# Log-sum-exp over rows of 1024: two rows of the last sixteen are summed partly through the logarithm of an early part

## The chip, the cores and the metric

The kernel runs on one core of a Trainium2 chip. The metric is the device time of one execution in microseconds (us). Five engines of the core appear in the profile: TensorE (PE), VectorE (DVE), ScalarE (ACT), GpSimd (POOL) and SyncE (SP), which here issues all transfers of the normal path. Each engine works through its own list of instructions in order and waits on semaphores for the others. Sixteen DMA engines move the data.

## The reference

```python
x: float32 [32, 512, 1024], standard normal
max_x = np.max(x, axis=-1, keepdims=True)
out = max_x.squeeze(-1) + np.log(np.sum(np.exp(x - max_x), axis=-1))   # float32 [32, 512]
```

So there are 16,384 rows of 1024 numbers, 67 MB to read and 64 KB to write.

## The kernel before

The kernel leaves the maximum out: it sums `exp(x)` as it is and takes the logarithm. A guard then decides whether that was allowed: it checks that the sums lie between 1e-15 and 1e15, adds up what is out of bounds in `count` with small matmuls, and only if the check fails does a branch (`nc.If`) read everything again and compute with the maximum. Of the last piece of data the guard looks at the numbers themselves (none over 27), so that it need not wait for their sum.

**Layout.** Each of the 128 partitions has 128 rows. The first 112 (`W`) of a partition lie in one stretch of memory, the last 16 (`B`) in another. "Columns" are numbers of one partition: a row is 1024 columns. Data land in `ring`, which holds 48 rows of a partition.

**Loads.** `LOADS` lists 18 loads by size in rows and by what is done with them. All are issued by SyncE in this order on one queue (line 143); a load waits until those who used its place in the ring are done. Nine loads carry the first 112 rows. Nine smaller ones carry the last 16: 4576, 3328, 2528, 1856, 1344, 992, 736, 544 and 480 columns.

**Work on a load.** ScalarE takes the exponentials in place (line 235). Rows marked R are summed by VectorE (line 246). Rows marked F are first folded to half by GpSimd (line 240), and VectorE sums the halves (line 177). Rows marked T, those of the last sixteen but one, are summed on VectorE by one instruction a row, which adds its two halves and accumulates (line 256). The last row comes in two pieces, Y (544 columns) and Z (480). For both ScalarE writes the exponentials to PSUM and accumulates their sum itself (line 209), into `first_sum` and `last_sum`. VectorE copies the first sum to SBUF (line 219).

**The end.** The logarithms of the first 112 rows are taken in the middle of the tail (line 275) and stored by line 285. At the end come the logarithms of 15 rows (line 288) and that of the last row (line 290), which adds the two halves through the bias:

```python
    ln_last = act.did(nc.scalar.activation(
        out=res[:, LAST:NC], in_=last_sum, func=AF.Ln, bias=sumexp[:, LAST:NC]
    ))
```

Line 294 stores these 16 columns. Beside it VectorE and TensorE finish the guard (lines 299 to 317); ScalarE and VectorE read its verdict and tell SyncE, which then waits for the store and ends the program.

Of the kernel before, what the change touches and what calls it, by code (L numbers as in the profile page):

```python
# [16 lines left out]
B = 16  # L17
LATE = 119
AHEAD = 1
FIRST = 512  # L20

LOADS = [
# [3 lines left out]
]  # L29

# [24 lines left out]
def kernel(  # L55
# [22 lines left out]
    W = NC - B  # L78
    LAST = NC - 1
    x_rows = x_flat[0 : P * W].rearrange("(p c) d -> p (c d)", p=P)  # L80
# [12 lines left out]
    ]  # L93
    assert sum(size for size, _ in loads) == NC * d
    assert sum(s for _, ops in loads for _, s in ops) == NC

# [3 lines left out]
    ring = sbuf("ring", RING * d)  # L100
    sumexp = sbuf("sumexp", NC)
    res = sbuf("res", NC)
    clamped = sbuf("clamped", NC)
    bad = sbuf("bad", 3)
    over = sbuf("over", d)
    far = sbuf("far", 1)
    ones = sbuf("ones", 1)
    steep = sbuf("steep", 1)
# [3 lines left out]
    first_sum = nc.alloc_psum_tensor("first_sum", [P, 1], fp32).ap()  # L112
# [3 lines left out]
    landed = [nc.alloc_semaphore(f"landed{i}") for i in range(len(loads))]  # L116
    act = Counted(nc, nc.scalar, "act")
# [12 lines left out]
    dve.did(nc.vector.memset(steep, STEEP))  # L130
    less_at = dve.did(nc.vector.memset(less, -CEILING * (loads[-1][0] // 2)))


# [15 lines left out]
    def check_early():  # L149
        dve.wait(act, summed_by_act)  # L150
        dve.wait(dve, dve.n)
        dve.did(nc.vector.tensor_scalar(  # L152
            out=clamped[:, 0:LATE], in0=sumexp[:, 0:LATE],
            scalar1=LOW, scalar2=HIGH, op0=ALU.max, op1=ALU.min,
        ))
        dve.wait(dve, dve.n)
        dve.did(nc.vector.scalar_tensor_tensor(  # L157
            out=clamped[:, 0:LATE], in0=clamped[:, 0:LATE], scalar=0.0, in1=sumexp[:, 0:LATE],
            op0=ALU.bypass, op1=ALU.not_equal, accum_out=bad[:, 0:1],
        ))  # L160
# [3 lines left out]
    def add_up(c, who, **kw):  # L164
        pe.wait(*who)
        return pe.did(nc.tensor.matmul(count, lhsT=ones, rhs=sumexp[:, c : c + 1], **kw))  # L166

    folded = []

    def reduce_folded():  # L170

        nonlocal early_sum
        while folded:
# [15 lines left out]
    summed_by_act = 0  # L189
    ln_early = None  # L190
    first_loads = []
    for i, (size, ops) in enumerate(loads):
        if here + size > RING * d:
            assert here == p
            p = here = 0
        if any(q < here + size and q + t * d > here for _, t, q, _ in folded):
            reduce_folded()
        dma = load(i, here, done_before, size)
        if i < AHEAD:
            first_loads.extend(x.ins for x in dma)  # L200
        end = here + size
        done_before += size
        act.wait(landed[i], 16 * len(dma))
        for k, (how, s) in enumerate(ops):
            rows = ring[:, p : p + s * d].rearrange("p (c d) -> p c d", d=d)
            if how in "YZ":

                assert c == LAST and (how == "Z" or here == p)
                at = act.did(nc.scalar.activation(  # L209
                    out=last_exp[:, here - p : end - p], in_=ring[:, here:end], func=AF.Exp,  # L210
                    accum_out=first_sum if how == "Y" else last_sum,
                ))
                if how == "Z":
                    last_piece = ring[:, here:end]
                here = end
                if how == "Y":
                    nc.vector.addr_align(128, offset=0, max_nops=0)
                    dve.wait(act, at)
                    first_piece = dve.did(nc.vector.tensor_copy(out=sumexp[:, LAST:NC], in_=first_sum))  # L219
                summed_by_act = at  # L220
            elif how == "A":
                assert here == p
                v = ring[:, p : p + d]
                at = act.did(nc.scalar.activation(
                    out=v, in_=v, func=AF.Exp, accum_out=sumexp[:, c : c + 1]
                ))
                here += d
                users.append((p, p + d, act, at))
                summed_by_act = at
                who = (act, at)  # L230
            else:

                upto = end if k + 1 == len(ops) and c + s < LAST else p + s * d
                v = ring[:, here:upto]
                at = act.did(nc.scalar.activation(out=v, in_=v, func=AF.Exp))  # L235
                here = upto
            if how == "F":
                reduce_folded()
                pool.wait(act, at)
                at = pool.did(nc.gpsimd.tensor_tensor(  # L240
                    out=rows[:, :, 0:H], in0=rows[:, :, 0:H], in1=rows[:, :, H:d], op=ALU.add
                ))
                folded.append((c, s, p, at))
            elif how == "R":
                dve.wait(act, at)
                who = (dve, dve.did(nc.vector.reduce_sum(  # L246
                    out=sumexp[:, c : c + s], in_=rows, axis=AX.X
                )))
                users.append((p, p + s * d, *who))
            elif how == "T":  # L250
                if c >= W:
                    reduce_folded()
                dve.wait(act, at)
                for r in range(s):
                    lo = rows[:, r, 0:H]
                    who = (dve, dve.did(nc.vector.scalar_tensor_tensor(  # L256
                        out=lo, in0=lo, scalar=1.0, in1=rows[:, r, H:d],
                        op0=ALU.mult, op1=ALU.add, accum_out=sumexp[:, c + r : c + r + 1],
                    )))
                    users.append((p + r * d, p + (r + 1) * d, *who))  # L260
                    if c + r >= LATE:
                        add_up(c + r, who, start=False, stop=False)
            if how == "A" and c >= LATE:
                add_up(c, who, start=False, stop=False)
            if how in "RT":
                if c < W:
                    early_sum = dve.n
                reduce_folded()
            c += s
            p += s * d  # L270
            if c == LATE:

                act.wait(dve, early_sum)
                act.wait(act, early_act)
                ln_early = act.did(nc.scalar.activation(  # L275
                    out=res[:, 0:W], in_=sumexp[:, 0:W], func=AF.Ln
                ))
                check_early()
            if c <= W:
                early_act = summed_by_act  # L280
        assert here == end

# [4 lines left out]
    act.wait(dve, dve.n)  # L287
    act.did(nc.scalar.activation(out=res[:, W:LAST], in_=sumexp[:, W:LAST], func=AF.Ln))  # L288
    act.wait(act, summed_by_act)
    ln_last = act.did(nc.scalar.activation(  # L290
        out=res[:, LAST:NC], in_=last_sum, func=AF.Ln, bias=sumexp[:, LAST:NC]
    ))
    sp.wait(act, ln_last)
    nc.sync.dma_start(out=out_rest, in_=res[:, W:NC]).then_inc(stored, 16)

    dve.wait(dve, dve.n)
    dve.did(nc.vector.scalar_tensor_tensor(  # L299
        out=clamped[:, LATE:NC], in0=sumexp[:, LATE:NC], scalar=LOW,  # L300
        in1=sumexp[:, LATE:NC], op0=ALU.max, op1=ALU.not_equal, accum_out=bad[:, 1:2],
    ))
    add_up(LAST, (dve, first_piece), start=False, stop=False)
# [4 lines left out]
    half = last_piece.shape[1] // 2  # L308
    dve.wait(landed[-1], 16)
    dve.did(nc.vector.scalar_tensor_tensor(  # L310
        out=over[:, 0:half], in0=last_piece[:, 0:half], scalar=CEILING,
        in1=last_piece[:, half : 2 * half], op0=ALU.max, op1=ALU.max, accum_out=bad[:, 2:3],
    ))
# [119 lines left out]
```

## Time and profile before

| | |
|---|---|
| median of 3 runs | 161.55 us (161.47 to 161.6) |
| the profiled execution | 161.57 us |
| its span, first to last instruction | 160.2 us |
| busy: VectorE | 114.3 us (71%) |
| busy: ScalarE | 114.5 us (71%) |
| busy: GpSimd | 37.3 us (23%) |
| busy: TensorE | 2.2 us (1%) |
| HBM read | 67.11 MB, 419 GB/s over the span |

Times in the profile count from the first instruction of the span. The page gives each engine's busy time, the span in 40 slices, the chain of work that ended last, and the costliest groups of instructions by line, engine, operation and shape. An engine's idle time is put down to what ended it. Two instructions of one engine can overlap: the next one starts before the one ahead of it has written its last result, so the pace of an engine is read from start to start. "SPq" is the list of SyncE, where transfers are issued.

### The profile page before, as it was taken

To read this page: it belongs to the slowest core of one execution; us is meant where nothing else is said; L and a number is where in the kernel's file an instruction comes from. 1 tells how busy PE (TensorE), PEld (TensorE's weight loads), DVE (VectorE), ACT (ScalarE), POOL (GpSimd) and SP (SyncE) were. 2 spreads that over 40 slices of the span, in tenths; PEclk is the share of its full clock that TensorE was granted. 3 is DMA by queue.
4 is the path that set the end of the run, shared out by engine and by line. 5 is a ranking of instruction groups with operands and counts; after the bars stand their busy time and mean duration, and the time that the engine had idled before them with its cause. 6 is when DMAs were issued, how large, how long until landed. Compare 5 with 4: busy or idle time off the path is not lost.

```text
span 160.2 us, 221 instructions
## 1 busy us (share of the span) xinstructions
PE 2.2 (1%) x26; PEld 1.1 (1%) x26; DVE 114.3 (71%) x59; ACT 114.5 (71%) x31; POOL 37.3 (23%) x11
## 2 busy tenths in 40 slices
PE   0000000000000000000000000000000000000022
PEld 0000000000000000000000000000000000000011
DVE  0000000009999499994999859959999999999996
ACT  3000059980799708995099949992999989799996
POOL 0000000000000000000000994690004969891000
DMA  9996996996996996997999999999999999999992
GB/s 319 507 460 301 507 524 262 524 524 262 524 524 262 524 524 262 524 474 311 483 442 442 442 425 409 409 409 471 423 414 417 458 409 399 444 412 428 415 408 97
DMA packets 3025, 67.18 MB, mean 419 GB/s; under 512 B 592, under 2 KB 720, under 8 KB 1488
## 3 DMA queue, kind: packets, MB, share of 16 engines
q1 hardware_dynamic: 3024, 67.18, 97.8%
q14 instruction: 1, 0.01, 0.0%
HBM read 67.11 MB, written 0.07 MB: 419 GB/s over the span
## 4 chain that ended last, share of the span: by engine, by line
DMA 51%; ACT 28%; DVE 19%; issue 1%; PE 0%
DMA ring<-in_x_dram 51%; ACT ring L235 28%; DVE sumexp L246 16%; DVE sumexp L177 2%; DVE ring L256 1%; DVE over L310 0%; PE count L315 0%; ACT res L275 0%; DVE clamped L299 0%; DVE fine L317 0%; DVE sumexp L219 0%
## 5 line engine op out<-in xcount | busy, mean ns | idle before, releaser
L235 ACT ACTIVATE ring<-ring 128x16384 f32<-128x16384 f32 (+16 forms) x23 | 111.7, 4908 | 42.3 <-DMA ring<-in_x_dram 42.3
L246 DVE TENSOR_REDUCE sumexp<-ring 128x16 f32<-128x16384 f32 (+4 forms) x9 | 85.6, 9513 | 42.1 <-ACT ring L235 42.1
L240 POOL TENSOR_TENSOR ring<-ring 128x3072 f32<-128x3072 f32 (+3 forms) x7 | 37.1, 5315 | 107.2 <-ACT ring L235 107.2
L177 DVE TENSOR_REDUCE sumexp<-ring 128x6 f32<-128x3072 f32 (+3 forms) x7 | 18.4, 2659 | 0.0
L256 DVE SCALAR_TENSOR_TENSOR ring<-ring 128x512 f32<-128x512 f32 x15 | 9.6, 687 | 0.4 <-ACT ring L235 0.4
L127 ACT ACT_TABLE_LOAD x1 | 1.3, 1283 | 1.9 <-PEq L64 1.9
L162 PE MATMUL count<-far,bad 128*1 128x1 f32 x2 | 0.2, 164 | 153.0 <-DVE clamped L157 153.0
L166 PE MATMUL count<-sumexp,ones 128*1 128x1 f32 x18 | 1.6, 164 | 3.6 <-DVE ring L256 3.6
L128 DVE MEMSET ones<- 128x1 f32 x1 | 0.1, 59 | 2.0 <-PEq L64 2.0
L256 DVE DVE_READ_ACCUMULATOR ring<-ring 128x1 f32 x15 | 1.2, 82 | 0.0
L209 ACT ACTIVATE last_exp<-ring 128x544 f32<-128x544 f32 (+1 forms) x2 | 1.2, 588 | 0.0
L162 PEld LDWEIGHTS count<-far,bad 128*1 128x1 f32 x2 | 0.1, 82 | 153.0 <-DVE clamped L157 153.0
L166 PEld LDWEIGHTS count<-sumexp,ones 128*1 128x1 f32 x18 | 0.8, 81 | 4.4 <-DVE ring L256 4.4
L310 DVE SCALAR_TENSOR_TENSOR over<-ring 128x240 f32<-128x240 f32 x1 | 0.4, 404 | 0.0
L317 DVE TENSOR_SCALAR fine<-count 1x1 int32<-1x1 f32 x1 | 0.1, 147 | 0.3 <-PE count L315 0.3
L157 DVE SCALAR_TENSOR_TENSOR clamped<-clamped,sumexp 128x119 f32<-128x119 f32 x1 | 0.3, 283 | 0.0
L275 ACT ACTIVATE res<-sumexp 128x112 f32<-128x112 f32 x1 | 0.3, 279 | 0.0
L290 ACT ACTIVATE res<-last_sum,sumexp 128x1 f32<-128x1 f32 x1 | 0.3, 261 | 0.0
L209 ACT ACTIVATION_READ_ACCUMULATOR last_exp<-ring 128x1 f32 x2 | 0.3, 129 | 0.0
L152 DVE TENSOR_SCALAR clamped<-sumexp 128x119 f32<-128x119 f32 x1 | 0.2, 222 | 0.0
L288 ACT ACTIVATE res<-sumexp 128x15 f32<-128x15 f32 x1 | 0.2, 213 | 0.0
L299 DVE SCALAR_TENSOR_TENSOR clamped<-sumexp 128x9 f32<-128x9 f32 x1 | 0.2, 170 | 0.0
(17 smaller groups left out, 1.8 us busy)
## 6 DMA issues: line engine op xcount, KB each, us to landing
ring<-in_x_dram SPq DMA_DIRECT2D x1, 7936.0 KB, 21.3
ring<-in_x_dram SPq DMA_DIRECT2D x1, 6912.0 KB, 23.9
ring<-in_x_dram SPq DMA_DIRECT2D x1, 6400.0 KB, 19.7
ring<-in_x_dram SPq DMA_DIRECT2D x1, 4608.0 KB, 15.9
ring<-in_x_dram SPq DMA_DIRECT2D x1, 3584.0 KB, 24.0
ring<-in_x_dram SPq DMA_DIRECT2D x1, 3072.0 KB, 19.1
ring<-in_x_dram SPq DMA_DIRECT2D x1, 2288.0 KB, 24.2
ring<-in_x_dram SPq DMA_DIRECT2D x1, 1664.0 KB, 20.9
```

Of the source, the lines that this page charges most:

```text
L127: nc.scalar.preload_act_table_set("natural_log_exp_and_others")
L157: dve.did(nc.vector.scalar_tensor_tensor(out=clamped[:, 0:LATE], in0=clamped[:, 0:LATE], scalar=0.0, in1=sumexp[:, 0:LATE], op0=ALU.bypass ...
L162: pe.did(nc.tensor.matmul(count, lhsT=bad[:, 0:1], rhs=far, start=True, stop=False))
L166: return pe.did(nc.tensor.matmul(count, lhsT=ones, rhs=sumexp[:, c : c + 1], **kw))
L177: at = dve.did(nc.vector.reduce_sum(out=sumexp[:, c0 : c0 + s0], in_=halves, axis=AX.X))
L209: at = act.did(nc.scalar.activation(out=last_exp[:, here - p : end - p], in_=ring[:, here:end], func=AF.Exp, accum_out=first_sum if how == ...
L235: at = act.did(nc.scalar.activation(out=v, in_=v, func=AF.Exp))
L240: at = pool.did(nc.gpsimd.tensor_tensor(out=rows[:, :, 0:H], in0=rows[:, :, 0:H], in1=rows[:, :, H:d], op=ALU.add))
L246: who = (dve, dve.did(nc.vector.reduce_sum(out=sumexp[:, c : c + s], in_=rows, axis=AX.X)))
L256: who = (dve, dve.did(nc.vector.scalar_tensor_tensor(out=lo, in0=lo, scalar=1.0, in1=rows[:, r, H:d], op0=ALU.mult, op1=ALU.add, accum_out ...
L275: ln_early = act.did(nc.scalar.activation(out=res[:, 0:W], in_=sumexp[:, 0:W], func=AF.Ln))
L310: dve.did(nc.vector.scalar_tensor_tensor(out=over[:, 0:half], in0=last_piece[:, 0:half], scalar=CEILING, in1=last_piece[:, half : 2 * half ...
```

## The change

The nine loads of the last sixteen rows are cut anew: 3760, 3488, 2656, 2000, 1456, 1088, 800, 608 and 528 columns. The order is no longer that of the memory. The last load, 528 columns (`HEAD`), is the first part of row 0; the one before it, 608 columns (`BACK`), is the last part of row 15. The other part of row 0 (496 columns) comes with the first late load, and that of row 15 (416 columns) with the second. The fourteen rows between are summed by VectorE as before, each when its columns are there.

The early parts of rows 0 and 15 are summed by VectorE into `parts`. A small logarithm on ScalarE turns each into ln(sum / 2) and writes it twice next to the place where the last piece of its row lands (`joins`; a gap of 32 columns in the ring makes room). The exponentials of the last two pieces run over these two columns too, so that the accumulator gets the early sum back (twice a half) and adds the rest. The sum of row 15 goes to `sumexp`, that of row 0 to `last_sum` in PSUM; neither last logarithm has a bias. The copy of the first sum is gone. The code place of VectorE that is aligned (`addr_align`) now stands ahead of the halves of the 800-column piece.

```diff
-    (9, "R5 F4"), (7, "F4 R3"), (6, "F2 F2 R2"), (4.46875, "T4"), (3.25, "T3"), (2.46875, "T3"),
-    (1.8125, "T2"), (1.3125, "T1"), (0.96875, "T1"), (0.71875, "T1"), (0.53125, "Y"), (0.46875, "Z"),
+    (9, "R5 F4"), (7, "F4 R3"), (6, "F2 F2 R2"),
 ]
+HEAD, BACK, MID = 528, 608, 12
+PIECES = [2656, 2000, 1456, 1088, 800]
...
+    start = MID * d - sum(PIECES)
+    late = [(HEAD, start), (MID * d, B * d - BACK)]
+    for size in PIECES:
+        late.append((start, start + size))
+        start += size
+    late += [(B * d - BACK, B * d), (0, HEAD)]
...
+    def halves(v, c):
+        n = v.shape[1] // 2
+        return dve.did(nc.vector.scalar_tensor_tensor(
+            out=v[:, 0:n], in0=v[:, 0:n], scalar=1.0, in1=v[:, n : 2 * n],
+            op0=ALU.mult, op1=ALU.add, accum_out=c,
+        ))
...
+    gap = p + (B - MID) * d
+    def place(e0):
+        return e0 - MID * d + p if e0 >= MID * d else gap + GAP + e0
+    joins = bass.AP(
+        tensor=ring.tensor, offset=ring[:, gap : gap + 1].offset,
+        ap=[ring.ap[0], [GAP - 2, 2], [1, 2]],
+    )
+    for k, (s, e) in enumerate(late):
+        i = len(loads) + k
+        at0, at1 = place(s), place(s) + e - s
+        [dma] = load(i, at0, W * d + s, e - s)
+        act.wait(landed[i], 16)
+        if k >= len(late) - 2:
+            act.wait(act, joined)
+        if k == len(late) - 1:
+            head_sum = act.did(nc.scalar.activation(
+                out=last_exp[:, 0 : e - s + 2], in_=ring[:, at0 - 2 : at1], func=AF.Exp,
+                accum_out=last_sum,
+            ))
+            break
+        if k == len(late) - 2:
+            v = ring[:, at0 : at1 + 2]
+            back_sum = act.did(nc.scalar.activation(
+                out=v, in_=v, func=AF.Exp, accum_out=sumexp[:, NC - 1 : NC]
+            ))
+            sums.append((NC - 1, act, back_sum))
+            add_up()
+            continue
+        v = ring[:, at0:at1]
+        at = act.did(nc.scalar.activation(out=v, in_=v, func=AF.Exp))
...
+        if k == len(late) - 3:
+            nc.vector.addr_align(128, offset=0, max_nops=0)
+        dve.wait(act, at)
+        seen.append((s, e))
...
+        if k == 0:
+            halves(ring[:, at0 : place(0) + d], parts[:, 1:2])
+        if k == 1:
+            halves(ring[:, place((B - 1) * d) : at1], parts[:, 0:1])
+            both = dve.n
+            act.wait(dve, early_sum)
+            ln_early = act.did(nc.scalar.activation(
+                out=res[:, 0:W], in_=sumexp[:, 0:W], func=AF.Ln
+            ))
+            check_early()
+        if k >= 1:
+            add_up()
+        if k == 2:
+            act.wait(dve, both)
+            joined = act.did(nc.scalar.activation(
+                out=joins, in_=parts[:, :, None].to_broadcast([P, 2, 2]), func=AF.Ln, scale=0.5
+            ))
...
     act.wait(dve, dve.n)
-    act.did(nc.scalar.activation(out=res[:, W:LAST], in_=sumexp[:, W:LAST], func=AF.Ln))
-    act.wait(act, summed_by_act)
-    ln_last = act.did(nc.scalar.activation(
-        out=res[:, LAST:NC], in_=last_sum, func=AF.Ln, bias=sumexp[:, LAST:NC]
+    act.wait(act, back_sum)
+    act.did(nc.scalar.activation(out=res[:, W + 1 : NC], in_=sumexp[:, W + 1 : NC], func=AF.Ln))
+    act.wait(act, head_sum)
+    act.did(nc.scalar.activation(out=res[:, W : W + 1], in_=last_sum, func=AF.Ln))
```

More of the change, by code (lines that the diff above doesn't have):

```diff
@@ L93 @@
     ]
-    assert sum(size for size, _ in loads) == NC * d
-    assert sum(s for _, ops in loads for _, s in ops) == NC
+    assert sum(size for size, _ in loads) == W * d
+    assert sum(s for _, ops in loads for _, s in ops) == W
+    start = MID * d - sum(PIECES)
[4 more added lines that the diff above has]
+    late += [(B * d - BACK, B * d), (0, HEAD)]
+    assert start == MID * d and sum(e - s for s, e in late) == B * d
     def sbuf(name, cols, dtype=fp32, rows=P):
@@ L130 @@
     dve.did(nc.vector.memset(steep, STEEP))
-    less_at = dve.did(nc.vector.memset(less, -CEILING * (loads[-1][0] // 2)))
+    less_at = dve.did(nc.vector.memset(less, -CEILING * (HEAD // 2)))
     users = []
@@ L162, in check_early, with add_up @@
         pe.did(nc.tensor.matmul(count, lhsT=bad[:, 0:1], rhs=far, start=True, stop=False))
-    def add_up(c, who, **kw):
-        pe.wait(*who)
-        return pe.did(nc.tensor.matmul(count, lhsT=ones, rhs=sumexp[:, c : c + 1], **kw))
+    sums = []
+    def add_up():
+        while sums:
+            c, who, at = sums.pop(0)
+            pe.wait(who, at)
+            pe.did(nc.tensor.matmul(
+                count, lhsT=ones, rhs=sumexp[:, c : c + 1], start=False, stop=False
+            ))
     folded = []
@@ L205 @@
             rows = ring[:, p : p + s * d].rearrange("p (c d) -> p c d", d=d)
[L206 to L236, printed above, removed]
+            upto = end if k + 1 == len(ops) else p + s * d
+            v = ring[:, here:upto]
+            at = act.did(nc.scalar.activation(out=v, in_=v, func=AF.Exp))
+            here = upto
             if how == "F":
@@ L243 @@
                 folded.append((c, s, p, at))
-            elif how == "R":
+            else:
                 dve.wait(act, at)
[L246 to L267, printed above, removed]
+                at = dve.did(nc.vector.reduce_sum(out=sumexp[:, c : c + s], in_=rows, axis=AX.X))
+                users.append((p, p + s * d, dve, at))
+                early_sum = at
                 reduce_folded()
@@ L270 @@
             p += s * d
[L271 to L280, printed above, removed]
-        assert here == end
+        assert here == end
+    assert c == W and here == p and p + GAP + B * d <= RING * d
@@ new lines @@
+    gap = p + (B - MID) * d
[5 more added lines that the diff above has]
+    )
+    summed = set()
+    seen = []
+    for k, (s, e) in enumerate(late):
[12 more added lines that the diff above has]
+        if k == len(late) - 2:
+            assert at1 == gap
+            v = ring[:, at0 : at1 + 2]
[6 more added lines that the diff above has]
+        v = ring[:, at0:at1]
+        at = act.did(nc.scalar.activation(out=v, in_=v, func=AF.Exp))
+        if k == 0:
+            reduce_folded()
+        if k == len(late) - 3:
+            nc.vector.addr_align(128, offset=0, max_nops=0)
+        dve.wait(act, at)
+        seen.append((s, e))
+        for r in range(1, B - 1):
+            left = r * d
+            for s0, e0 in sorted(seen):
+                if s0 <= left < e0:
+                    left = e0
+            if r not in summed and left >= (r + 1) * d:
+                summed.add(r)
+                row = ring[:, place(r * d) : place(r * d) + d]
+                sums.append((W + r, dve, halves(row, sumexp[:, W + r : W + r + 1])))
+        if k == 0:
+            halves(ring[:, at0 : place(0) + d], parts[:, 1:2])
[13 more added lines that the diff above has]
+                out=joins, in_=parts[:, :, None].to_broadcast([P, 2, 2]), func=AF.Ln, scale=0.5
+            ))
```

35 lines of the change are left out of this document (16 added, 19 removed).

## The prediction

> **What bounds the kernel now.** I read the page first: is this kernel short of transfers or of an engine?
>
> ```profile
> span 160.2 us, 221 instructions
> ...
> DMA  9996996996996996997999999999999999999992
> ...
> DMA 51%; ACT 28%; DVE 19%; issue 1%; PE 0%
> ```
>
> The transfers are busy in nearly every slice, and in all of the second half. The change leaves the first nine loads as they are, so only what follows the six-row load matters. Hence the timeline of ScalarE, one instruction at a time, from there to the end:
>
> ```profile
> 138.06 1.91 ACT L235 ACTIVATE ring<-ring 128x2048 f32<-128x2048 f32 x1 [1.02 <-DMA ring<-in_x_dram]
> 141.68 1.89 ACT L235 ACTIVATE ring<-ring 128x2048 f32<-128x2048 f32 x1
> 143.51 4.02 ACT L235 ACTIVATE ring<-ring 128x4576 f32<-128x4576 f32 x1
> 147.44 2.98 ACT L235 ACTIVATE ring<-ring 128x3328 f32<-128x3328 f32 x1
> 150.33 0.28 ACT L275 ACTIVATE res<-sumexp 128x112 f32<-128x112 f32 x1
> 150.51 2.29 ACT L235 ACTIVATE ring<-ring 128x2528 f32<-128x2528 f32 x1
> 152.73 1.75 ACT L235 ACTIVATE ring<-ring 128x1856 f32<-128x1856 f32 x1
> 154.39 1.32 ACT L235 ACTIVATE ring<-ring 128x1344 f32<-128x1344 f32 x1
> 155.62 1.02 ACT L235 ACTIVATE ring<-ring 128x992 f32<-128x992 f32 x1
> 156.54 0.80 ACT L235 ACTIVATE ring<-ring 128x736 f32<-128x736 f32 x1
> 157.25 0.61 ACT L209 ACTIVATE last_exp<-ring 128x544 f32<-128x544 f32 x1
> 157.85 0.57 ACT L209 ACTIVATE last_exp<-ring 128x480 f32<-128x480 f32 x1
> 158.34 0.13 ACT L209 ACTIVATION_READ_ACCUMULATOR last_exp<-ring 128x1 f32 x1
> 158.39 0.21 ACT L288 ACTIVATE res<-sumexp 128x15 f32<-128x15 f32 x1
> 158.51 0.26 ACT L290 ACTIVATE res<-last_sum,sumexp 128x1 f32<-128x1 f32 x1
> ```
>
> From 138.06 ScalarE shows no idle time. That alone could mean that it is the bound. So I looked at when its data landed: the issues of SyncE in the timeline and, for the same loads, the time from issue to landing in the DMA view.
>
> ```profile
> 126.47 0.33 SPq L143 DMA_DIRECT2D ring<-in_x_dram  x1
> 135.53 0.33 SPq L143 DMA_DIRECT2D ring<-in_x_dram  x1
> 136.37 0.43 SPq L143 DMA_DIRECT2D ring<-in_x_dram  x1
> 136.85 1.54 SPq L143 DMA_DIRECT2D ring<-in_x_dram  x1
> 158.79 0.34 SPq L294 DMA_DIRECT2D out_dram<-res  x1
> ```
>
> ```profile
> ring<-in_x_dram SPq DMA_DIRECT2D x1, 272.0 KB, 20.8
> ring<-in_x_dram SPq DMA_DIRECT2D x1, 240.0 KB, 20.9
> out_dram<-res SPq DMA_DIRECT2D x1, 8.0 KB, 1.4
> ```
>
> The 544 columns landed at 136.37 + 20.8 = 157.17 and the last 480 at 136.85 + 20.9 = 157.75; their exponentials started at 157.25 and 157.85. So the two race: ScalarE is under 0.1 us behind the transfers. Does it keep its own pace? Two groups of the table by form give it:
>
> ```profile
> L235 ACT ACTIVATE ring<-ring 128x16384 f32<-128x16384 f32 x3 | 41.6, 13856 | 29.6 <-DMA ring<-in_x_dram 29.6
> L235 ACT ACTIVATE ring<-ring 128x4576 f32<-128x4576 f32 x1 | 4.0, 4017 | 0.0
> ```
>
> (13.856 - 4.017) / 11,808 columns is 0.8333 ns per column. From start to start 736 columns took 157.25 - 156.54 = 0.71 us, 0.10 over the columns; the log of 112 took 0.18, 0.09 over. I take a step as 0.8333 ns per column + 0.095 us. With an accumulator it is 0.147 over: 157.85 - 157.25 = 0.60 for 544. By this the 1856 columns could have started at 150.51 + 2.20 = 152.71 and did at 152.73; 1344, at 154.37 and did at 154.39. Transfers and ScalarE are tied within some 0.02 us at every step; gaining on one alone gains nothing.
>
> The last store is issued at 158.79, right behind the last log (158.51 + 0.26 = 158.77), and lands 1.4 later, at 160.2: the end of the span. The page's chain ends on VectorE's guard, which I check against SyncE's waits:
>
> ```profile
> SPq L376 <- ACTq L373: 0.7, 1, 0.7
> SPq L378 <- SPq L378: 0.3, 1, 0.3
> ```
>
> After its issue (158.79 + 0.34) SyncE waits 0.7 for the guard's verdict, then 0.3 for the store. So the guard has 0.3 us to spare. The profiled execution took 161.57 us, 1.33 over its span, and 0.02 over the median of 161.55. 0.2% of that, 0.32 us, is about what a measurement of this kernel can tell from no change.
>
> **The change part by part.** *Loads.* The last sixteen rows were nine loads of 4576, 3328, 2528, 1856, 1344, 992, 736, 544 and 480 columns; they become nine of 3760, 3488, 2656, 2000, 1456, 1088, 800, 608 and 528. Bytes and number are the same, so I cost the last landing at nothing: 157.75. The new first piece lies about four rows further along the ring, and waits for the reduction behind the 126.47 issue; the fifth piece now carries the wait behind the 135.53 issue. Their cover is the queue: nothing of the late pieces can move before the six-row load is in (138.06), 11 us later. Without that cover a late issue would delay every landing one for one.
>
> *Where the pieces start.* Before, four of nine pieces (3328, 2528, 736 and 480) start 128 bytes past a multiple of 256; after, six do not start at one (64, 128, 192, 128, 128 and 128 past), and a gap of 128 bytes shifts seven destinations against their sources. From one start on ScalarE to the next is what the later piece took to arrive, as the two are tied: 147.44 - 143.51 = 3.93 us for the 3328, 1.18 ns per column, and 0.92 for the 736, 1.25; beside them 2.22 for 1856 columns that start at a multiple, 1.20, and 1.23 for 992, 1.24. The shifted ones do not stand out, so I take nothing. The Trainium skill ("DMA: Bandwidth & Descriptors", "How a descriptor splits into AXI transactions") says that a read that does not begin at a multiple of 256 bytes also fetches the bytes from that boundary on, and pays for them. By it the starts wasted 4 x 128 = 512 bytes per partition before and 64 + 192 + 4 x 128 = 768 after, 32 KB more in all, an estimate of 0.08 us at the rate of the late pieces (8.39 MB in 19.7 us): a rule against the change, which the rows above don't bear out.
>
> *ScalarE's list.* Interpolating ScalarE's starts by columns gives when each new piece is there: 3760 at 142.54, then 146.67, 149.87, 152.27, 154.05, 155.40, 156.40, and from the two landings 157.11 and 157.75 (with 0.03 to start). Its list: the three 2048s of the six-row load end their steps at 141.68 + 1.80 = 143.48, so the 3760 wait 0.9 us for ScalarE. Then steps of 3.23 (to 146.71), 3.00 (149.71), the early log 0.19 (149.90), 2656 in 2.31 (152.21), the new small log 0.10 (152.31), 2000 in 1.76 (154.07), 1456 in 1.31 (155.38; data 155.40), 1088 in 1.00 (156.40), 800 in 0.76 (157.16), and 610 with an accumulator in 0.508 + 0.147 (157.82). Its data would be there at 157.78. So the last exponentials start at 157.82, 0.03 earlier than 157.85; they have 530 columns for 480, 0.04 more; accumulator read at 158.35 instead of 158.34.
>
> *The small log and its wait.* It stands in front of the 2000-column exponentials and waits for VectorE's sum of row fifteen's part. What is queued behind it is all that ScalarE still has to do. VectorE's rows:
>
> ```profile
> 146.38 1.22 DVE L177 TENSOR_REDUCE sumexp<-ring 128x2 f32<-128x1024 f32 x1
> 147.56 0.69 DVE L256 SCALAR_TENSOR_TENSOR ring<-ring 128x512 f32<-128x512 f32 x1
> 148.18 0.69 DVE L256 SCALAR_TENSOR_TENSOR ring<-ring 128x512 f32<-128x512 f32 x1
> 158.28 0.40 DVE L310 SCALAR_TENSOR_TENSOR over<-ring 128x240 f32<-128x240 f32 x1
> 158.60 0.08 DVE L310 DVE_READ_ACCUMULATOR over<-ring 128x1 f32 x1
> ```
>
> A row costs 0.62 us, 240 columns 0.32, so about 1.1 ns per column: 0.33 for the 248 of row zero, 0.29 for the 208 of row fifteen. Rows one to three and the part of row zero: 147.56 + 1.86 + 0.33 = 149.75. The 3488 end at 146.71 + 3.11 = 149.82; from 149.85 three rows and a part take 2.15, plus 0.08 for the accumulator: 152.08. ScalarE wants it at 152.21, so the wait costs nothing by 0.13 us. Its price is 0.10 as a step; from above it is bounded by the whole duration of the 112-column log, 0.28, if nothing overlaps it. I take 0.10, since that row's own step was 0.18. Below 0.09 it cannot go.
>
> *The 608's accumulator* now goes to the sums beside its row instead of PSUM: between 0 and one uncovered read, 0.13; I take 0, as the read before it overlapped. It also waits for two things, its data and the small log; ScalarE has no row for that. It is bounded by 0 and by the 0.08 from the landing at 157.17 to the start at 157.25; I take 0, the small log being 4.8 us old by then.
>
> *VectorE's end.* The copy of the first half's sum goes, and the last row's halves are those of the 800. The 1456's exponentials end at 154.07 + 1.21 + 0.20 = 155.48, and behind them four rows of 0.62 follow one another, the last two not held up by the 1088 (end 156.51) or the 800 (157.27): 157.96, with the read 158.04. The remaining logs want them at 158.40; the guard's final maximum starts no later than now (158.28) and is 24 columns, 0.03, longer. The 0.3 us of the guard hide this.
>
> *The last logs.* Fifteen columns at 158.40, the last one 0.12 later at 158.52. With the bias it took 0.26. The fifteen-column log without one took 0.21, of which 0.01 is columns: 0.20, a gain of 0.06. It could be 0, if reading the sum from PSUM is what costs; at most 0.10, as the exponentials that touch PSUM have the shortest fixed part (0.61 - 0.45 = 0.16). I take 0.06. The Trainium skill ("ScalarE: Activation LUTs", "What ACT_TABLE_LOAD costs") gives about 93 ns for a bias read per partition; by it the end would be 0.03 us earlier still.
>
> *Sum.* -0.03 (start) + 0.04 (columns) - 0.06 (bias) = -0.05 us: store issued at 158.74, span near 160.19, profiled execution 161.52, median 161.50.
>
> **The rivals.** *One: ScalarE's list grows* (slower). Its list and the landings tie, so whatever its steps cost more from 152.2 on comes out at the end one for one. Place: small log and 608. Price: small log not overlapped 0.18, accumulator 0.13, second wait 0.08, bias worth nothing 0.06: together 0.45, so 161.50 + 0.45 = 161.95. It passes 0.32 over the median when about 0.37 of this is real, or if VectorE's part is there after 152.6. For it: no row shows these forms, and ScalarE has no idle time to lose. Against: reads and short logs overlapped in every row.
>
> *Two: the starts cost* (the page's rule). Landing at 157.83, last start 157.86: 0.04 over the forecast, 161.54. Against: no misaligned row stands out.
>
> *Three: the transfers get faster,* from the shifted destinations. For it, the windows show room:
>
> ```profile
> 130.00:136.00 6.00, 0.00 (x0) 0.00 (x0) 6.00 (x3) 5.46 (x3) 5.70 (x2) 1.00 1.01 434
> 155.00:157.00 2.00, 0.61 (x8) 0.26 (x6) 1.97 (x7) 2.00 (x3) 0.00 (x0) 1.00 0.99 391
> ```
>
> The tail moves 391 GB/s where large pieces moved 434. The late pieces (16,384 columns of 4 bytes on 128 partitions, 8.39 MB) took 157.75 - 138.06 = 19.7 us; at 434 they take 19.3, 0.36 less. Against: ScalarE's list holds the start at about 157.8, so 161.48 is the price; a real gain of 0.36 (161.14) would need shorter steps as well. A fourth way, that the guard fails on the new sums and all is read again, would double the time; it gets 1%, counted with rival one.
>
> **How the numbers follow.** Forecast 0.63 (161.35 to 161.65: the three runs spread over 0.13, and single prices are uncertain by about 0.1). Rival one at its full size 0.20. Rival two 0.07, within 0.2%. Rival three 0.10, nearly all of the chance of faster, since it needs what no row shows. Faster by over 0.2%: 0.09. Within: 0.71. Slower: 0.20. The range goes from half of rival three's gain, 161.30, to just short of rival one's sum, 161.92.
>
> **What would show it.** Right: 530 columns starting near 157.82 with their read near 158.35; the small log near 152.2, starting without idle time and followed 0.10 later; the last log at 0.20; the store issued near 158.74. Wrong: idle time before the small log, with VectorE as its releaser; a step of the 610 columns above 0.66; the last landing away from 157.75; SyncE's last wait being the guard's and not the store's.

## The result, and the profile after

The changed kernel takes **161.99 us** in the median of ten runs (161.83 to 162.24), the kernel before 161.54 beside it (161.47 to 161.63, ten runs): a ratio of 1.0028, with a 95% interval of 1.0018 to 1.0037. It is slower by 0.45 us, where 161.50 with a range up to 161.92 was forecast.

The page of the changed kernel, its span, transfers by slice and the chain by engine:

```profile
span 160.1 us, 250 instructions
...
DMA  8995996996996996997999999999999999999993
...
DMA 51%; ACT 27%; DVE 20%; issue 0%; PE 0%
```

The span did not grow: 160.14 us in this execution, against 160.24 before. But the execution took 161.83 us. Outside its span lie 161.83 - 160.14 = 1.69 us; before it was 161.57 - 160.24 = 1.33. The profile after, read alone, would say that the change gained a tenth of a microsecond.

Over all executions with a span and a time it is the same: time less span has a mean of 1.70 us for the changed kernel (ten runs, 1.65 to 1.74) and 1.35 for the kernel before (33 runs, 1.29 to 1.39). The two sets do not touch. Spans are 160.29 and 160.22 in the mean, and vary by some tenths from run to run in both. So 0.35 of the 0.45 us lies outside the span. The other 0.1 is not steady: two kernels of the experiments below that execute what the changed kernel does, `e6` and `e14`, have mean spans of 160.21 and 160.22, with 160.22 for the kernel before beside each.

Now ScalarE's timeline after, for the stretch that the prediction worked out (start, duration; a row with x2 to x4 is that many exponentials in one group):

```profile
137.97 5.51 ACT L226 ACTIVATE ring<-ring 128x2048 f32<-128x2048 f32 x3 [1.04 <-DMA ring<-in_x_dram]
143.38 6.32 ACT L280 ACTIVATE ring<-ring 128x3760 f32<-128x3760 f32 x2
149.61 0.28 ACT L302 ACTIVATE res<-sumexp 128x112 f32<-128x112 f32 x1
149.80 2.40 ACT L280 ACTIVATE ring<-ring 128x2656 f32<-128x2656 f32 x1
152.10 0.19 ACT L310 ACTIVATE ring<-sumexp 128x4 f32<-128x4 f32 x1
152.20 5.01 ACT L280 ACTIVATE ring<-ring 128x2000 f32<-128x2000 f32 x4
157.11 0.70 ACT L273 ACTIVATE ring<-ring 128x610 f32<-128x610 f32 x1
157.71 0.19 ACT L273 ACTIVATION_READ_ACCUMULATOR ring<-ring 128x1 f32 x1
157.81 0.59 ACT L265 ACTIVATE last_exp<-ring 128x530 f32<-128x530 f32 x1
158.34 0.12 ACT L265 ACTIVATION_READ_ACCUMULATOR last_exp<-ring 128x1 f32 x1
158.39 0.20 ACT L321 ACTIVATE res<-sumexp 128x15 f32<-128x15 f32 x1
158.50 0.17 ACT L323 ACTIVATE res<-last_sum 128x1 f32<-128x1 f32 x1
```

This execution runs 0.09 us ahead of the one before: its six-row exponentials start at 137.97 and not at 138.06. With that put back, the small log starts at 152.19 (forecast 152.21), the 2000 columns at 152.29 (152.31), the 610 at 157.20 (157.16), the 530 at 157.90 (157.82). The last log takes 0.17 where it took 0.26. From the landing of the six-row load to the end of the span both executions take 22.20 us (22.18 to 22.20 in the experiments `e1`, `e3`, `e6` and `e14` below, in which ScalarE executes the same list): inside the span the change is worth nothing.

The parts of VectorE and SyncE that the prediction leaned on, first VectorE's timeline, then SyncE's, then SyncE's waits (who <- whom: total, times, longest):

```profile
151.58 0.37 DVE L199 SCALAR_TENSOR_TENSOR ring<-ring 128x208 f32<-128x208 f32 x1
151.88 0.08 DVE L199 DVE_READ_ACCUMULATOR ring<-ring 128x1 f32 x1
...
157.90 0.08 DVE L199 DVE_READ_ACCUMULATOR ring<-ring 128x1 f32 x1
...
158.12 0.43 DVE L340 SCALAR_TENSOR_TENSOR over<-ring 128x264 f32<-128x264 f32 x1
```

```profile
158.69 0.34 SPq L325 DMA_DIRECT2D out_dram<-res  x1
```

```profile
SPq L406 <- ACTq L403: 0.7, 1, 0.7
SPq L408 <- SPq L408: 0.4, 1, 0.4
```

Row fifteen's part is summed at 151.96, the small log starts at 152.10: the wait costs nothing. The guard's maximum starts at 158.12, before it was 158.28; SyncE still waits last for its store, not for the guard. The store is issued 0.10 earlier than before (158.69 against 158.79), the 0.09 of this execution's head start.

### The profile page after: what moved, and what is told of

It is laid out like the page before. It is cut to its first block, busy times and chain, and to the rows that moved or that the text cites. A ratio compares the mean times of both kernels' runs of the same rounds, so it can differ in the third digit from the quotient of the medians.

```text
span 160.1 us, 250 instructions
## 1 busy us (share of the span) xinstructions
PE 2.5 (2%) x38; PEld 1.3 (1%) x38; DVE 114.2 (71%) x60; ACT 114.5 (71%) x32; POOL 37.3 (23%) x11
## 4 chain that ended last, share of the span: by engine, by line
DMA 51%; ACT 27%; DVE 20%; issue 0%; PE 0%
DMA ring<-in_x_dram 51%; ACT ring L226 19%; DVE sumexp L237 16%; ACT ring L280 7%; DVE sumexp L190 2%; DVE ring L199 2%; DVE over L340 0%; PE count L345 0%; ACT res L302 0%; DVE clamped L330 0%; DVE fine L347 0%; ACT ring L310 0%
## 5 line engine op out<-in xcount | busy, mean ns | idle before, releaser
L226 ACT ACTIVATE ring<-ring 128x16384 f32<-128x16384 f32 (+9 forms) x16 | 98.0, 6169 | 42.3 <-DMA ring<-in_x_dram 42.3
L280 ACT ACTIVATE ring<-ring 128x3760 f32<-128x3760 f32 (+6 forms) x7 | 13.7, 2006 | 0.0
L199 DVE SCALAR_TENSOR_TENSOR ring<-ring 128x512 f32<-128x512 f32 (+2 forms) x16 | 9.6, 652 | 0.4 <-ACT ring L280 0.3
L273 ACT ACTIVATE ring<-ring 128x610 f32<-128x610 f32 x1 | 0.7, 696 | 0.0
L265 ACT ACTIVATE last_exp<-ring 128x530 f32<-128x530 f32 x1 | 0.6, 595 | 0.0
```

The costliest lines, as they stand in the source:

```text
L199: return dve.did(nc.vector.scalar_tensor_tensor(out=v[:, 0:n], in0=v[:, 0:n], scalar=1.0, in1=v[:, n : 2 * n], op0=ALU.mult, op1=ALU.add, ...
L265: head_sum = act.did(nc.scalar.activation(out=last_exp[:, 0 : e - s + 2], in_=ring[:, at0 - 2 : at1], func=AF.Exp, accum_out=last_sum,))
L273: back_sum = act.did(nc.scalar.activation(out=v, in_=v, func=AF.Exp, accum_out=sumexp[:, NC - 1 : NC]))
```

## The experiments

The question is what makes 0.35 us that no row of the profile holds. The change alters what each engine is given to execute: by the compiled programs, ScalarE has 60 instructions where it had 57 (the small log and the second wait of two instructions that now wait twice), VectorE 85 for 83, TensorE 87 for 63 (six more sums are added up, each two weight loads and two matmuls), GpSimd and SyncE as many as before. Each ratio below is to the kernel before, run beside it on the same chip.

### First: TensorE's list (theory A), or VectorE's jump to an aligned place (theory B)

`e1_after_pe63`, the changed kernel with TensorE's list cut back to 63; the guard does not add up six of the last rows:

```
 def add_up():
         c, who, at = sums.pop(0)
+        if c - W in (1, 2, 3, 12, 13, 14):
+            continue
```

> The changed kernel with six of its fifteen small matmuls left out (rows 1, 2, 3, 12, 13, 14 are not checked against the upper bound; the output is the same), so that TensorE has 63 instructions as before the change, not 87. Theory A (the lost time lies outside the span and comes from TensorE's longer list): time minus span falls from 1.7 to 1.33 us, the span stays at 160.1 to 160.3, time 161.5 to 161.6. Theory B (VectorE's jump to its aligned code place now comes 0.9 us earlier) and theory C (the longer lists of ScalarE, 57 to 60, and VectorE, 83 to 85): no difference, 162.0, 1.7 outside the span.

Measured: 161.97, ratio 1.0021 [1.0012, 1.0030], 1.70 outside the span.

`e2_before_pe87`, the kernel before with TensorE's list as long as after's, and `e4_before_pe75`, half way (`range(3)`); the guard adds six (three) sums twice:

```
 def check_early():
+    for c in range(6):
+        pe.did(nc.tensor.matmul(count, lhsT=ones, rhs=sumexp[:, c : c + 1], start=False, stop=False))
```

> The kernel before with six more small matmuls (sums of columns 0 to 5 are added to the guard's count once more), 87 instructions on TensorE as in the changed kernel. Theory A: span unchanged at 160.2, 1.7 outside it, time 161.9. Theories B and C: 161.55, 1.33 outside the span.

> The kernel before with three more small matmuls, 75 instructions on TensorE. Theory A as a step (a block of code more to load): either 161.55 with 1.33 outside the span, or 161.9 with 1.7. Theory A in proportion (24 instructions cost 0.36, 15 ns each): 161.73 with 1.51 outside. Theories B and C: 161.55.

Measured: 161.58, ratio 1.0001 [0.9992, 1.0010], 1.34 outside; and 161.57, 0.9998 [0.9989, 1.0007], 1.35 outside.

`e3_after_jump_late`, the changed kernel with the jump at the place in VectorE's list that follows all row sums:

```
-        if k == len(late) - 3:
-            nc.vector.addr_align(128, offset=0, max_nops=0)
...
+    nc.vector.addr_align(128, offset=0, max_nops=0)
     dve.wait(dve, dve.n)
```

> The changed kernel with VectorE's aligned code place moved back behind the last row's halves. Theory A: as the changed kernel, 162.0 and 1.7 outside the span. Theory B: 161.6 and 1.33. Theory C: 162.0.

Measured: 161.88, ratio 1.0025 [1.0016, 1.0034], 1.71 outside. What follows: A falls from both sides, since TensorE's list neither brings the loss nor, cut back, takes it away. B falls: the jump's place does nothing.

### Second: ScalarE's code (C1) or VectorE's (C2), without executing any of it

The guard's branch, in which all is read again, is not entered with these inputs, but its instructions stand in each engine's program. So an engine's list can be made longer with nothing more executed. `e5_before_act60`, `e8_before_act58` and, further below, `e17_before_act63` and `e13_before_act69` put 3, 1, 6 and 12 logs into ScalarE's part of that branch, ahead of its last log; `e7_before_dve86` puts three memsets into VectorE's:

```
+        for _ in range(3):
+            nc.scalar.activation(out=far, in_=ones, func=AF.Ln)
```

> The kernel before with three more instructions on ScalarE inside the branch that is never taken (logs of a constant): 60 instructions on its list as in the changed kernel, none of them executed. Theory C1 (the length of ScalarE's list costs the time outside the span, executed or not): 161.9 us, 1.70 outside the span. Theory C2 (VectorE's list, 83 to 85) and theory D (something that is executed: the small log, the doubled waits): 161.55, 1.35 outside.

> The kernel before with three more instructions on VectorE inside the never-taken branch, 86 on its list (83 before, 85 in the changed kernel). Theory C2: 161.9, 1.70 outside the span. Theories C1 and D: 161.55, 1.35.

> The kernel before with one more instruction on ScalarE inside the never-taken branch: 58. Theory C1 as a step: either 1.35 or 1.70 outside the span and nothing between; in proportion: 1.47 (0.12 per instruction). Theories C2 and D: 1.35, 161.55.

`e6_after_act56` is the changed kernel without the last log, the stores and the waits of ScalarE in that branch, 56 instructions (what the branch would compute is not stored):

```
-        nc.scalar.wait_ge(ready, steps)
-        nc.scalar.activation(out=res, in_=sumexp[:, 0:NC], func=AF.Ln).then_inc(ready, 1)
...
-        nc.scalar.dma_start(out=out_rest, in_=res[:, W:NC]).then_inc(again, 16)
-        nc.scalar.dma_start(out=out_rows, in_=res[:, 0:W]).then_inc(again, 16)
-        nc.scalar.wait_ge(again, rows + 32)
```

> The changed kernel with four instructions of ScalarE's part of the never-taken branch left out (its last log and stores), 56 on its list; all that is executed is as in the changed kernel. Theory C1: 161.55 to 161.6, 1.35 outside the span. Theories C2 and D: 162.0, 1.70 outside.

Measured: e5 161.94, ratio 1.0027 [1.0018, 1.0037], 1.71 outside; e6 161.57, 0.9998 [0.9988, 1.0007], 1.38; e7 161.66, 1.0001 [0.9990, 1.0011], 1.36; e8 161.59, 1.0005 [0.9994, 1.0015], 1.34. The page and ScalarE's timeline of e5:

```profile
span 160.1 us, 221 instructions
```

```profile
157.75 0.56 ACT L209 ACTIVATE last_exp<-ring 128x480 f32<-128x480 f32 x1
158.24 0.13 ACT L209 ACTIVATION_READ_ACCUMULATOR last_exp<-ring 128x1 f32 x1
158.29 0.21 ACT L288 ACTIVATE res<-sumexp 128x15 f32<-128x15 f32 x1
158.41 0.26 ACT L290 ACTIVATE res<-last_sum,sumexp 128x1 f32<-128x1 f32 x1
```

These are the same 221 recorded instructions as before and the same last logs, in a span of 160.1 us. Yet this execution too took 161.83 us. Three instructions that are never executed cost all that the change cost outside the span, and with four fewer in the branch the changed kernel is rid of it (e6). C2 falls; the cause is in ScalarE's list. How it depends on the list is the next question.

### Third: does the length decide, or the place where ScalarE's code ends (theory P)? And do starts of pieces matter inside the span?

`e9_after_act58` is the whole change with two of ScalarE's waits saved: the early log of 112 rows goes behind the 2000 columns and needs no wait on VectorE of its own, and the last logs wait for VectorE's final check, which covers their second wait:

```
-            act.wait(dve, early_sum)
-            ln_early = act.did(nc.scalar.activation(out=res[:, 0:W], in_=sumexp[:, 0:W], func=AF.Ln))
...
+        if k == 3:
+            act.wait(act, joined)
+            ln_early = act.did(nc.scalar.activation(out=res[:, 0:W], in_=sumexp[:, 0:W], func=AF.Ln))
...
-    act.wait(dve, dve.n)
-    act.wait(act, back_sum)
+    act.wait(dve, checked)
```

> The changed kernel, complete, with ScalarE's list shortened from 60 to 58 by saving its two doubled waits: the early log of 112 columns moves behind the 2000 columns and waits for the small log there, and the last logs wait for VectorE's final check, which has itself waited for row fifteen's sum. Theory C1 (a block of code is exceeded between 58 and 60): 1.35 outside the span, time 161.55 to 161.6. If the doubled waits or the small log as executed cost the time: 161.9 or more only if the log matters, as the waits are gone.

Measured: 161.62, ratio 1.0005 [0.9996, 1.0014], 1.36 outside. With a shorter list the change's loss is gone.

`e13_before_act69` (the branch with 12 more logs):

> The kernel before with twelve more instructions of ScalarE in the never-taken branch: 69. Theory C1 as a step: 1.70 outside the span as with 60, 161.9. As a price per instruction beyond 58: 0.18 each, 3.3 outside, 163.5.

Measured: 161.60, ratio 1.0003 [0.9993, 1.0013], 1.35 outside. Twelve more instructions leave the time as it was, where three cost 0.35: it does not grow with the length. They are not without effect, though. SyncE's wait for ScalarE's word on the guard, in e13:

```profile
SPq L378 <- ACTq L375: 1.0, 1, 1.0
```

In the kernel before it was 0.7, and a wait of 0.3 for the store followed; here none is left for the store. In the trace ScalarE's signal comes 0.42 us after the start of its jump over the branch, where it was 0.16 in the kernel before. And an instruction transfer of 8,192 bytes starts 0.42 us behind the end of the span, as in no run with 63 instructions or fewer. So with 69 ScalarE is held up by some 0.27 us where it passes over the branch. That lies inside the span, and the store's landing hides it.

`e10_after_act58_aligned` is e9 with all pieces starting at multiples of 256 bytes in memory, and `e12_before_aligned` the same for the kernel before:

```
-HEAD, BACK, MID = 528, 608, 12
-PIECES = [2656, 2000, 1456, 1088, 800]
+HEAD, BACK, MID = 512, 640, 12
+PIECES = [2624, 1984, 1472, 1088, 832]
```

```
-    ... (4.46875, "T4"), (3.25, "T3"), (2.46875, "T3"),
-    (1.8125, "T2"), (1.3125, "T1"), (0.96875, "T1"), (0.71875, "T1"), (0.53125, "Y"), (0.46875, "Z"),
+    ... (4.5, "T4"), (3.25, "T3"), (2.5, "T3"),
+    (1.8125, "T2"), (1.3125, "T1"), (0.9375, "T1"), (0.6875, "T1"), (0.5, "Y"), (0.5, "Z"),
```

> The same with pieces of 3776, 3456, 2624, 1984, 1472, 1088, 832, 640 and 512 columns, each starting at a multiple of 256 bytes. From the landing of the six-row load to the last landing the trace has 19.71 to 19.73 us for the kernel before and 19.75 to 19.77 for the changed one. Theory R (starts off a multiple of 256 bytes cost what the page's rule says, scaled to the 0.05 seen for 256 bytes per partition): 768 bytes fewer, 19.61. Theory S (the 0.05 come from the sizes or from the shifted destinations): 19.75 to 19.77 still. Time by R: 161.45, as ScalarE's list holds its end near 157.8; by S 161.55.

> The kernel before with the late pieces 4608, 3328, 2560, 1856, 1344, 960, 704, 512 and 512, each starting at a multiple of 256 bytes (before: four start 128 past one). Theory R: 19.72 falls by 0.10 to 19.62. Theory S: 19.72. Time: within 0.1 of 161.52 by both, since ScalarE's last piece grows by 32 columns (0.03).

Measured: e10 161.56, ratio 1.0001 [0.9992, 1.0010]; e12 161.69, 1.0008 [0.9999, 1.0017]. From the landing of the six-row load to the last landing e10 took 19.53 us (e9 19.74), but e12 19.92 (before 19.73): aligned starts went with 0.2 less in one kernel and 0.2 more in the other, so a start in memory does not by itself set the rate. (The new cuts also change the sizes and the places in the ring: with the ring where it is, all nine pieces of e12 land 128 bytes past a multiple of 256, two in e10.) ScalarE's timeline of e10 shows why its 0.2 were worth nothing:

```profile
138.07 1.91 ACT L226 ACTIVATE ring<-ring 128x2048 f32<-128x2048 f32 x1 [1.03 <-DMA ring<-in_x_dram]
...
157.22 0.72 ACT L273 ACTIVATE ring<-ring 128x642 f32<-128x642 f32 x1
157.85 0.19 ACT L273 ACTIVATION_READ_ACCUMULATOR ring<-ring 128x1 f32 x1
157.94 0.58 ACT L265 ACTIVATE last_exp<-ring 128x514 f32<-128x514 f32 x1
```

Its last piece had landed at 157.57 and was begun at 157.94, when ScalarE came to it: 19.87 after the six-row start, against 19.84 in the changed kernel (157.81 - 137.97). Rival three's cover, that ScalarE's list holds the end, is seen here.

### Fourth: theory P on the changed kernel, and the ring's own place (theory D)

`e14_after_act69` is the changed kernel, complete, with nine logs in the branch that is not entered; `e17_before_act63` gives one more point.

```
+        for _ in range(9):
+            nc.scalar.activation(out=far, in_=ones, func=AF.Ln)
```

> The changed kernel with nine more instructions of ScalarE in the never-taken branch, 69 on its list. Theory P (the place: the time outside the span is lost when the end of ScalarE's list stands at certain places, so at 60 but not at 56, 57, 58 or 69): 1.35 outside the span, 161.6. Theory C1 as a length: 1.70 and 162.0.

> The kernel before with six more instructions of ScalarE in the never-taken branch: 63. It looks for the far end of the bad places: 1.70 outside the span if they reach from 59 or 60 to 63 or more, 1.35 if they are narrower.

Measured: e14 161.53, ratio 0.9996 [0.9986, 1.0005], 1.32 outside; e17 161.59, 1.0003 [0.9993, 1.0013], 1.42 outside (1.38 to 1.44). In e14 SyncE's wait for ScalarE shows the same as in e13:

```profile
SPq L408 <- ACTq L405: 0.9, 1, 0.9
```

All together, time less span by the length of ScalarE's list: 56 1.38, 57 1.34 to 1.36 (six kernels), 58 1.34 to 1.36 (four), **60 1.70, 1.70, 1.71 and 1.71**, 63 1.42, 69 1.35 and 1.32. Four kernels with 60 and none else have the loss of 0.35. With 63 it is 0.07, which the expectation had not foreseen; 59, 61 and 62 were not tried.

`e15_before_ring256` moves the ring in SBUF by 128 bytes, so that it begins at a multiple of 256 (byte 16640 instead of 16512). The buffers behind it move along, so the run does not tell the ring's place from theirs; nothing else differs from the kernel before:

```
+    sbuf("pad", 32)
     ring = sbuf("ring", RING * d)
```

> The kernel before with the ring moved by 128 bytes (an unused tensor of 32 columns ahead of it), so that it starts at a multiple of 256 bytes of a partition and not 128 past one. Theory D (a load costs some 0.05 us more when its destination does not start at a multiple of 256 bytes; from the late pieces: 2 off 19.53, 5 off 19.72, 6 off 19.76, 9 off 19.92): all nine early loads and one more late one are in place, 0.5 us less, 161.0 to 161.1, and 19.66 from the six-row load's landing to the last. Theory S (sizes and sources): 161.55 and 19.72.

Measured: **161.30**, ratio 0.9985 [0.9976, 0.9994], 1.34 outside: faster than the kernel before by 0.15%, with an interval that leaves out 1. Its page and ScalarE's timeline:

```profile
span 160.0 us, 221 instructions
```

```profile
21.77 13.86 ACT L236 ACTIVATE ring<-ring 128x16384 f32<-128x16384 f32 x1 [18.57 <-DMA ring<-in_x_dram]
...
137.78 1.91 ACT L236 ACTIVATE ring<-ring 128x2048 f32<-128x2048 f32 x1 [0.96 <-DMA ring<-in_x_dram]
...
157.57 0.56 ACT L210 ACTIVATE last_exp<-ring 128x480 f32<-128x480 f32 x1
```

From the first exponentials, which start with the first load's landing, to the six-row ones it is 137.78 - 21.77 = 116.01 us; before, the first row was

```profile
21.79 13.86 ACT L235 ACTIVATE ring<-ring 128x16384 f32<-128x16384 f32 x1 [18.58 <-DMA ring<-in_x_dram]
```

and the six-row ones started at 138.06: 116.27. In the traces of the sixteen kernels that leave the ring in its place, it took 116.24 to 116.30 from landing to landing. The gain of 0.26 us lies in these eight loads, not in the engines' work: 16,384 columns take ScalarE 13.86 us in both. It has theory D's sign and some half of its size. The late pieces took 19.66, as D said.

`e16_best` joins e10, the moved ring and a gap of 256 bytes, so that every piece also ends up at a multiple of 256 in the ring:

```
-GAP = 32
+GAP = 64
...
+    sbuf("pad", 32)
```

> The changed kernel with 58 instructions on ScalarE, pieces at multiples of 256 bytes, the ring moved by 128 bytes and the gap of 64 columns, so that every source and every destination starts at a multiple of 256 bytes. Theory D: nine early loads give 0.45 us, the late pieces land at 19.42 but ScalarE's list holds the end: 161.1. Theory S: 161.55.

Measured: 161.50 (161.27 to 162.01), ratio 1.0001 [0.9991, 1.0011], 1.34 outside. Its early loads took as long as e15's (116.00 from landing to landing), but its late pieces 19.65, not less than e10's 19.53 without the moved ring. Theory D said 19.42. So the early loads get shorter in both runs with the moved ring, but D does not give the late pieces; what sets those (19.53, 19.65, 19.66, 19.74, 19.92 in e10, e16, e15, e9, e12) stays open. And in its profiled run the end of the span is 22.22 after the six-row landing, as in e10 (22.20) and the kernel before (22.20): what its late transfers gain, ScalarE's list holds back. That run also lost 0.2 us before its first exponentials, which started at 21.97 where e15's did at 21.77; why its executions spread by 0.74 us is not known. The only version that was measurably faster than the kernel before is e15.

## Why the prediction was wrong

**The step that failed** stands in the sum: the span "near 160.19" was turned into a time by the 1.33 us that the execution before had "over its span", taken as a constant. The span was right within its spread (160.14 in the profiled execution); the 1.33 became 1.69. Of the 0.31 us by which the profiled execution missed its 161.52, this term is 0.36 and the span -0.05. No row of the profile before gives this term or what it depends on, but the prediction did not bound it either, and none of its rivals names it. The range's upper end, 161.92, and the chance of 0.20 for slower came from rival one's sum; 161.99 lies above it for another reason, and that the prediction allowed for slower was luck. Rival one itself, a longer ScalarE list *inside* the span, did not happen: ScalarE's list did cost, but by where its code ends.

**What is shown and what is not.** Shown: the loss is outside the span (1.70 against 1.35); three never-executed ScalarE instructions bring it to the kernel before (e5), nine more or four fewer take it from the changed one (e14, e6). Not shown is the mechanism, since that part of an execution has no rows, nor whether the 0.35 us lies ahead of the span or behind it. The events outside the span that the traces hold do not tell the kernels apart: the last semaphore event comes 1.46 us behind the span's end in the kernel before, in the changed kernel and in e5. One reading would fit: code arrives in blocks, and with 60 instructions an edge between two blocks falls among or behind the last that ScalarE executes. With 69 it would fall ahead of them, where ScalarE passes over the branch: there e13 and e14 show it held up by 0.27 us, hidden behind the store. The Trainium skill ("Runtime: NRT & Kernel Launch", "Instruction fetch mechanics") says that an engine's code is fetched in blocks of 256 instructions, that a crossing is mostly hidden, and that a branch to code outside what was fetched stalls until it has come. By that figure a list of 60 holds an edge only if it does not begin at one, and no run shows where it begins. In these traces one instruction transfer, of 8,192 bytes, lies in the span, 1.17 us behind VectorE's jump, in both kernels. The delay with 69 looks like such a stall; that the 0.35 us with 60 are a crossing that is not hidden is argued, not shown, and the 0.07 with 63 is not explained.

**The terms inside the span**, by the prediction's own steps:
- *Bias*, put at 0.06: the last log went from 0.261 to 0.169, so 0.09. The Trainium skill's figure for such an operand ("ScalarE: Activation LUTs", "What ACT_TABLE_LOAD costs": about 93 ns) was the better one; the trace agrees with it.
- *The 608's accumulator*, put at 0: its step, 157.11 to 157.81, was 0.69 by the trace's finer times where 0.655 was worked out, and above the 0.66 that the prediction named as a sign of being wrong. Its read, into SBUF, takes 0.19, where reads into PSUM take 0.12 and 0.13, and the next instruction starts 0.10 after this read has begun (157.71 to 157.81; 157.85 to 157.94 in e10), but 0.05 after a read into PSUM (158.34 to 158.39; 158.24 to 158.29 in e5). Of the bound of 0.13, 0.04 is real.
- *Late pieces*, put at no change: 19.77 us from landing to landing, and 19.74 to 19.78 in the runs with these pieces, against 19.70 to 19.73 in those with the pieces before. That is 0.05, rival two's sign and about its 0.04 at the end. It told at the 610 columns: they started 19.14 us after the six-row exponentials, where 157.16 - 138.06 = 19.10 was worked out. The last 528 had landed at 157.71 and waited for ScalarE until 157.81. That rival two's rule does it is not borne out: e12, with every start aligned, took 19.92, though its destinations moved too. What the Trainium skill says of reads off a multiple of 256 bytes ("DMA: Bandwidth & Descriptors", "How a descriptor splits into AXI transactions") does not order these times.
- *The sum:* -0.05 was forecast. Accumulator +0.04, late data +0.05 and the bias 0.03 better give -0.05 + 0.06 = +0.01; measured is 0.00 (22.20 from the six-row landing to the end, both times).
- *Right:* the small log neither waits nor adds more than 0.10; the margin of 0.13 by which VectorE is early was 152.10 - 151.96 = 0.14; the guard stayed hidden; the 50 more columns cost their 0.04.

Rival three, faster transfers from other destinations, did not come in this change. Yet e15 has 0.26 us of something like it, from a ring that begins 128 bytes further on, in loads that the change does not touch.

## What to carry to other kernels

Subtract the span from the measured time for both kernels before reading any row; if the difference lies outside, no wait in the profile explains it. Where an edit changes how many instructions an engine has, waits and never-taken branches included, pad that engine's list by a few unexecuted instructions and measure again, before the edit is called slow. And try another start for a large DMA destination: here one line of padding, which put it at a multiple of 256 bytes, gained 0.24 us, where the change gained nothing. Whether it is the multiple that counts was not tested with other places.

## What the runs showed of the hardware

- Code that is never executed cost 0.35 us of 161.5, and more of it took that away again: with 60 instructions on ScalarE 1.70 us lay outside the span, with 63 1.42, with 57 1.35, with 69 1.35 and 1.32.
- With 69, ScalarE's signal came 0.42 us after the start of its jump over the branch, with 57 0.16.
- Moving the ring, and the buffers behind it, by 128 bytes took the eight loads from the first landing to the six-row one from 116.27 to 116.01 us.
- An accumulator read into SBUF took 0.19 us on ScalarE, into PSUM 0.12 and 0.13.
